# Stacked attention operands by per-block copies and doubled transposes, and half of a softmax's scalings on ScalarE, in a hybrid encoder layer

## The chip, the cores and the metric

The kernel runs on one core of one Trainium2 chip. The metric is the device time of one execution, in microseconds (us). TensorE (PE) multiplies matrices, VectorE (DVE) and ScalarE (ACT) do elementwise work, GpSimd (POOL) here raises small vectors to a power and issues DMA transfers that can add to what lies in the destination, and SyncE (SP) issues plain DMA loads.

## The reference

One layer of a bidirectional encoder on 512 tokens of width 1024, in float32. A vector `c` gives shift, scale and gate for three sublayers:

```python
x = x + 0.5 * g1 * swiglu(modulate(rmsnorm(x)), w_ffn1_in, w_ffn1_out)
h = modulate(rmsnorm(x))
qa, ka, va, qb, kb, vb, ga, gb = split(h @ w_in)
# mixer A: 8 query heads, 2 key heads of 64, keys within 128 positions, a sink in the softmax
ya = window_gqa_sink(rope(rmsnorm(qa)), rope(rmsnorm(ka)), va, sink) @ w_branch_a
# mixer B: 4 heads, two softmaxes each (64 wide), softmax_0 - lam * softmax_1, values 128 wide
yb = rmsnorm(diff_attention(rope(rmsnorm(qb)), rope(rmsnorm(kb)), vb, lam)) * 0.8 @ w_branch_b
x = x + g2 * ((sigmoid(ga) * ya + sigmoid(gb) * yb) @ w_out)
x = x + 0.5 * g3 * swiglu(modulate(rmsnorm(x)), w_ffn2_in, w_ffn2_out)
```

## The kernel before

All big products are made in a split form. A float32 operand is held as a high part, rounded to the format that TensorE multiplies, and a low part, the rest. A product is then three matmuls: high by high, high by low, low by high. `split_from` (L168) makes the parts: ScalarE copies the source to the high part (L169), VectorE subtracts to get the low part (L170). `load_split` (L194) does this for a weight of 128 by 1024 that SyncE has loaded into a `raw` tile. `load_main` (L1063) does it otherwise: ScalarE writes the high part (L1068) and the negated high part into the low tile (L1069), and a GpSimd DMA (L1070) adds the same weight from DRAM to it, so VectorE has no part in it. Weights in split form stand in one of five places (`high_low`, L175), which a holder can reserve.

The scores of both mixers use stacked operands instead. A head is 64 wide, and TensorE contracts over 128 partitions. One operand carries the high part of a head on partitions 0 to 63 and its low part on partitions 64 to 127; the other carries a head doubled. Two matmuls with full height then do what three would do with half height (L1293, L1451).

The middle of the kernel works like this. `main` (L1543) is a stream of projections, gate products and branch products, and yields an estimated cost after each step. `Line` (L47) keeps an estimated clock and a list of pieces of attention work with due times; when the clock passes a due time, the piece is put into the program there. Pieces also ask that a PSUM bank be free by the estimate (`line.free`). In this part the order on each engine is not the program's: a scheduler with its own model of times orders the instructions by what is ready. Buffers are tiles with a tag and a fixed number of slots; a tile that finds no free slot waits. PSUM banks: three of tag "acc", three of "sc", one "tp", one "op".

- `project` (L1116) multiplies the normalised input with a projection's weight into four banks (three "acc", one "sc"), one for each block of 128 tokens.
- `keys_b` (L1236): for each of four blocks, `keys` (L1209) norms and rotates the keys, and `turn_heads` (L1191) transposes four pairs of heads on TensorE (`turned`, L1179, in the bank "tp") and splits the result. So `kb[0]` first holds high parts of both heads of a pair (on partitions 0 to 63 and 64 to 127), and `kb[1]` the low parts. After the last block three GpSimd copies, each of 64 partitions by 2048 elements (512 KB), exchange halves by way of a spare tile (L1242 to L1244), each after the one before: then `kb[0]` holds high and low part of the first heads, `kb[1]` those of the second.
- `queries_b` (L1254), which follows the next projection, doubles the queries by a ScalarE copy; `query_turn` (L1265) transposes them, and `diff_scores` (L1278) runs the score products, 16 units in all, with gate products (`gates`, L1140) as filler work between the pieces.
- `queries_a` (L1420): for each of four blocks the queries of mixer A are transposed and split into two tiles of tag "f2" (eight slots), and four GpSimd copies of 64 partitions by 512 elements (128 KB, L1427) put high and low parts of each key head's queries into `wa["q"]`. After block 0 the first window scores are due 5.5 us after the estimate of the bank "tp" being free.
- `window_scores` (L1437), eight units of four score products, each followed by a softmax: scores with the mask (L1454), the maximum and the sink (L1465 to L1468), four exponentials on ScalarE (L1471), sums and reciprocals (L1475, L1476), and four scalings by the reciprocal on VectorE (L1478). `window_turn` transposes the probabilities, `window_out` multiplies with the values.
- Beside the window stage run the rest of the gates, the branch of mixer B (`w_yb`), and the first half of the branch of mixer A (`w_ya`, tokens 0 to 255, L1539); its second half waits until all window units are done. `load_ya` (L1573) loads the four weights of `w_ya` by `load_split` and keeps them for both halves.

Then come the product with `w_out`, and the second SwiGLU, where the order is written out by hand.

Of the kernel before, what the change touches and what calls it, by code (L numbers as in the profile page):

```python
# [18 lines left out]
P = 128  # L19
# [105 lines left out]
def layer(ctx: ExitStack, tc: tile.TileContext, a: dict):  # L125
# [934 lines left out]

    hh, hl = new_h()

    def load_main(src):  # L1063

        raw = sbuf("raw", [P, 1024], F32, RAW)
        nc.sync.dma_start(raw, src)
        hi, lo = high_low()
        S.copy(hi, raw)  # L1068
        S.activation(lo, raw, AF.Identity, scale=-1.0)  # L1069
        G.dma_start(lo, src, accum_op=ALU.add)  # L1070
        return hi, lo
# [119 lines left out]
    def turn_heads(srcs, hi, lo):  # L1191
        v = turned(srcs).rearrange("p (j q) -> p j q", j=len(srcs))
        split_from(hi, lo, v)

    def raws(ps, n=T):
# [3 lines left out]
            S.copy(out[-1], p[:, 0:n])  # L1199
        return out  # L1200

    def queries(ps, tabs, rq, outs, then):
        for t, raw in enumerate(raws(ps)):
            z = head_stats(raw, 8, rq[:, t, :], True)
            y = rope(raw, 8, tabs, t, z, outs and outs[t])
            due = line.helped(2.6, 2.5) + SLACK
            line.at(due, lambda y=y, t=t: then(y, t), ("tp",))
# [27 lines left out]

    def keys_b(ps):  # L1236
        def then(y, ht):
            hi, lo = kb
            turn_heads(cut(y, 4), hi[:, :, ht], lo[:, :, ht])
            if ht.stop == T:  # L1240
                spare = ob_h[0:HD]
                G.dma_start(spare, hi[HD:P])  # L1242
                G.dma_start(hi[HD:P], lo[0:HD])
                G.dma_start(lo[0:HD], spare)  # L1244

        for t, raw in enumerate(raws(ps)):
            keys(raw, 8, table["kb"], t, then)
# [172 lines left out]
    def queries_a(ps):  # L1420
        def then(y, t):
            ht = slice(t * P, (t + 1) * P)
            both = [sbuf("f2", [P, 4, P], F32R, F2) for _ in range(2)]
            turn_heads(cut(y, 4), *both)
            for kv in range(2):
                for j in range(2):
                    G.dma_start(wa["q"][kv][j * HD : (j + 1) * HD, :, ht], both[j][kv * HD : (kv + 1) * HD])  # L1427
            if t == 0:
                line.at(line.free["tp"] + 5.5, lambda: window_scores(0, 0, 0, None), ("sc0", "sc1"))

        queries(ps, table["qa"], wa["rq"], None, then)

# [4 lines left out]
    def window_scores(b, kv, g, st):  # L1437
        rqa = wa["rq"]
        first, nk = span(b)
        n = nk * P  # L1440
        mo = (first - (b - 1)) * P
        bq = slice(b * P, (b + 1) * P)
        bk = slice(first * P, first * P + n)
        unit = 2 * b + kv
        if g == 0:
            wide = b8(F32) if unit % 3 == 2 else None
            st = (small(4), [], line.now, wide)
        mx, sc, start, wide = st
        s_ps = bank("sc")
        for j in range(2):  # L1450
            PE.matmul(s_ps[:, 0:n], wa["q"][kv][:, g, bq], wa["k"][j][:, kv, bk], start=j == 0, stop=j == 1)  # L1451
        line.now += MM3 * 2 / 3 * n / T
        s = xt() if wide is None else wide[:, g, :]
        V.tensor_tensor_reduce(  # L1454
            out=s[:, 0:n], in0=s_ps[:, 0:n], in1=wa["mask"][:, mo : mo + n], scale=1.0, scalar=TINY,
            op0=ALU.add, op1=ALU.max, accum_out=mx[:, g : g + 1],
        )
        line.free[f"sc{(4 * unit + g) % 3}"] = line.helped(0.5, 0.3)
        sc.append(s)
        if g < 3:  # L1460
            line.at(line.now, lambda: window_scores(b, kv, g + 1, st), (f"sc{(4 * unit + g + 1) % 3}",))
            return
        den, nm, es = small(4), small(4), small(4)
        sk = sink[:, kv * 4 : kv * 4 + 4]
        V.tensor_tensor(nm, mx, rqa[:, b, kv:8:2], ALU.mult)  # L1465
        V.tensor_tensor(nm, nm, sk, ALU.max)
        V.tensor_tensor(es, sk, nm, ALU.subtract)
        V.tensor_scalar(nm, nm, -1.0, None, ALU.mult)  # L1468
        S.activation(es, es, AF.Exp)
        for q in range(4):  # L1470
            S.activation(  # L1471
                sc[q][:, 0:n], sc[q][:, 0:n], AF.Exp, bias=nm[:, q : q + 1],
                scale=rqa[:, b, 2 * q + kv : 2 * q + kv + 1], accum_out=den[:, q : q + 1],
            )
        V.tensor_tensor(den, den, es, ALU.add)  # L1475
        V.reciprocal(den, den)  # L1476
        for q in range(4):
            V.tensor_scalar(sc[q][:, 0:n], sc[q][:, 0:n], den[:, q : q + 1], None, ALU.mult)  # L1478
        due = line.helped(0.5, 3.2)
        due = line.helped(1.3, 0.5, due)  # L1480
        line.at(due + SLACK, lambda: window_turn(b, kv, 0, sc), (turn_tag(b, kv, 0),))
        nxt = (b, 1) if kv == 0 else (b + 1, 0)
        if nxt[0] < NT:
            line.at(
                start + PERIOD_A, lambda: window_scores(*nxt, 0, None),
                (f"sc{(4 * unit + 4) % 3}", lambda: unit - turns["a"] < DEPTH_A),
            )
# [55 lines left out]
    def main():  # L1543
        yield from project(vb_w, T, values_b)
        yield from project(a["w_kb"], T, keys_b, load_split, 1)
        yield from project(a["w_qb"], T, queries_b, load_split, 2)
        yield from gates(lambda: done["b"] < NT)
        line.drain(lambda: done["b"] == NT)
        start_a()
        again()  # L1550
        yield from project(a["w_kva"], 256, keys_a, load_half, 3)
        yield from project(a["w_qa"], T, queries_a, load_split, 3)
        yield from gates()
        ma = [b8(F32) for _ in range(2)]

        def then_a(j, g, y, r):
            V.scalar_tensor_tensor(ma[j // 4][:, j % 4, r], g, 1.0, y, ALU.add, ALU.mult)
            line.helped(0.6)

        yield from branch(a["w_yb"], 8, ob_h, ob_l, then_a, load_main)  # L1560
        mix.extend(new_h())
        mh, ml = mix

        def then_b(j, g, y, r):
            V.scalar_tensor_tensor(g, g, 1.0, y, ALU.add, ALU.mult)
            m = ma[j // 4][:, j % 4, r]
            V.tensor_tensor(m, m, g, ALU.add)
            split_from(mh[j][:, r], ml[j][:, r], m)
            line.helped(1.0)

        w_ya = {}

        def load_ya(u):  # L1573
            if u in w_ya:
                let_go(("ya", u))
            else:
                w_ya[u] = load_split(a["w_ya"][u], aside=ASIDE, holder=("ya", u))
            return w_ya[u]

        for i, r in enumerate(HALVES):  # L1580
            line.drain(lambda: done["a"] >= 2 * i + 2)
            yield from branch(range(4), 0, *wa["o"], then_b, load_ya, r)
# [377 lines left out]
```

## Time and profile before

| | |
|---|---|
| median of 3 runs | 1082.35 us (1080.17 to 1082.73) |
| the profiled execution's own time | 1081.27 us |
| span of its trace | 1079.5 us |
| mean granted TensorE clock | 0.99 |
| PE busy | 1046.5 us (97%), 7184 matmuls |
| VectorE busy | 801.4 us (74%) |
| ScalarE busy | 572.5 us (53%) |
| GpSimd busy | 155.8 us (14%) |
| DMA | 215.65 MB, mean 200 GB/s |

The profile shows one execution. A row of the timeline gives start, duration, engine, line, operation, output and input names, and in brackets the engine's idle time before it with what ended that. Rows of the waits give who waited for whom: total, number of times, longest. The granted clock is the share of TensorE's full clock. Rows of POOL's or SP's DMA instructions are the issues; a transfer lands later. "DMA b<-b" in a wait is a transfer's landing.

### The profile page before, as it was taken

How to read it: one execution, taken by the hardware profiler on the slowest of the kernel's cores; microseconds unless marked ns; L12 is line 12 of the kernel's file. 1: busy time of each engine (PE TensorE's matmuls, PEld its weight loads, DVE VectorE, ACT ScalarE, POOL GpSimd, SP SyncE). 2: the span in 40 equal slices, each digit the busy share in tenths (PEclk: the TensorE clock that was granted, in tenths of full speed). 3: DMA queues.
4: the chain of work that ended last, by engine and by line, in shares of the span. 5: the costliest groups of instructions: out<-in, count | busy, mean ns of one | idle time of the engine just before them, and what ended most of it. 6: DMA issues, size and time to landing. Idle time of an engine off the chain costs nothing.

```text
span 1079.5 us, 18400 instructions
## 1 busy us (share of the span) xinstructions
PE 1046.5 (97%) x7184; PEld 956.2 (89%) x7184; DVE 801.4 (74%) x1449; ACT 572.5 (53%) x938; POOL 155.8 (14%) x181
## 2 busy tenths in 40 slices
PE   8999999999999999979999899899999999999998
PEld 6799899889998988857887778789999999999997
DVE  7987877687867755647963589885878777877877
ACT  5566235425554534658645366434765645655553
POOL 1100001010101102411002700101021111211210
PEclk9999999999999999989999999899999999999999
DMA  9967887697776294963458961884397999998974
GB/s 350 372 154 227 270 211 188 200 278 203 177 220 216 101 350 121 207 149 89 124 175 198 230 164 61 304 286 79 78 206 172 235 240 238 184 231 210 222 150 122
DMA packets 68777, 215.65 MB, mean 200 GB/s; under 512 B 7953, under 2 KB 14225, under 8 KB 68498
## 3 DMA queue, kind: packets, MB, share of 16 engines
q1 hardware_dynamic: 43920, 143.63, 39.0%
q0 software_dynamic: 22320, 66.60, 34.1%
q10 hardware_dynamic: 2450, 4.25, 1.1%
q8 instruction: 56, 0.92, 0.3%
q14 instruction: 31, 0.25, 0.1%
HBM read 201.86 MB, written 8.92 MB: 195 GB/s over the span
## 4 chain that ended last, share of the span: by engine, by line
PE 73%; issue 8%; DVE 7%; DMA 6%; ACT 3%; POOL 2%; ACTq 0%; SPq 0%; DVEq 0%; POOLq 0%
PE acc L434 5%; PE acc L435 5%; PE acc L436 5%; PE sc L166 5%; PE sc L165 5%; PE sc L164 5%; PE sc L434 5%; PE sc L436 5%; PE sc L435 5%; PE acc L165 2%; PE acc L164 2%; PE acc L166 2%; PE acc L1132 2%; PE acc L1134 2%; PE acc L1133 2%
## 5 line engine op out<-in xcount | busy, mean ns | idle before, releaser
L434 PE MATMUL acc<-b,high 128*128 128x256 f32 x614 | 170.7, 278 | 0.4 <-DVE f L504 0.2
L436 PE MATMUL acc<-b,low 128*128 128x256 f32 x614 | 170.5, 278 | 0.1
L435 PE MATMUL acc<-b,high 128*128 128x256 f32 x614 | 170.4, 278 | 0.2 <-DVE b L1744 0.2
L169 ACT CAST high<-raw 128x1024 fp32r<-128x1024 f32 (+1 forms) x92 | 94.6, 1032 | 120.1 <-PE sc L1134 19.0
L434 PE MATMUL sc<-b,high 128*128 128x256 f32 x550 | 152.4, 277 | 1.3 <-ACT f L502 1.2
L436 PE MATMUL sc<-b,low 128*128 128x256 f32 x550 | 152.4, 277 | 0.1
L435 PE MATMUL sc<-b,high 128*128 128x256 f32 x550 | 152.1, 277 | 0.0
L170 DVE TENSOR_TENSOR low<-raw,high 128x1024 fp32r<-128x1024 f32 (+1 forms) x92 | 109.9, 1199 | 51.4 <-ACT high L169 51.0
L434 PEld LDWEIGHTS acc<-b,high 128*128 128x128 f32 x614 | 115.8, 189 | 0.8 <-DVE f L504 0.4
L435 PEld LDWEIGHTS acc<-b,high 128*128 128x128 f32 x614 | 116.0, 189 | 0.5 <-DVE b L1744 0.4
L436 PEld LDWEIGHTS acc<-b,low 128*128 128x128 f32 x614 | 115.8, 189 | 0.4 <-DVE low L170 0.3
L434 PEld LDWEIGHTS sc<-b,high 128*128 128x128 f32 x550 | 103.3, 188 | 1.7 <-ACT f L502 1.7
L436 PEld LDWEIGHTS sc<-b,low 128*128 128x128 f32 x550 | 103.3, 188 | 0.5 <-DVE low L786 0.3
L435 PEld LDWEIGHTS sc<-b,high 128*128 128x128 f32 x550 | 103.3, 188 | 0.0
L164 PE MATMUL sc<-b,high 128*128 128x512 f32 (+1 forms) x272 | 99.1, 364 | 0.0
L166 PE MATMUL sc<-b,low 128*128 128x512 f32 (+1 forms) x272 | 98.8, 363 | 0.2 <-DVE low L880 0.2
L165 PE MATMUL sc<-b,high 128*128 128x512 f32 (+1 forms) x272 | 99.0, 364 | 0.0
L169 ACT CAST high<-u 128x1024 fp32r<-128x1024 f32 (+1 forms) x51 | 52.2, 1025 | 44.3 <-PE acc L435 12.3
L164 PE MATMUL acc<-b,high 128*128 128x512 f32 (+1 forms) x200 | 74.4, 374 | 0.7 <-ACT b L169 0.7
L165 PE MATMUL acc<-b,high 128*128 128x512 f32 (+1 forms) x200 | 73.1, 366 | 0.0
L166 PE MATMUL acc<-b,low 128*128 128x512 f32 (+1 forms) x200 | 73.0, 365 | 0.0
L170 DVE TENSOR_TENSOR low<-u,high 128x1024 fp32r<-128x1024 f32 (+1 forms) x51 | 60.8, 1191 | 15.2 <-ACT high L169 14.6
(387 smaller groups left out, 2705.2 us busy)
## 6 DMA issues: line engine op xcount, KB each, us to landing
u<-w_mod SPq DMA_DIRECT2D x66, 512.0 KB, 7.1
raw<-w2i SPq DMA_DIRECT2D x31, 512.0 KB, 5.3
u<-w2i POOLq DMA_DIRECT2D x31, 512.0 KB, 7.0
raw<-w1u SPq DMA_DIRECT2D x27, 512.0 KB, 5.1
u<-w1u POOLq DMA_DIRECT2D x18, 512.0 KB, 8.0
raw<-w1o SPq DMA_DIRECT2D x16, 512.0 KB, 3.9
raw<-w_gate SPq DMA_DIRECT2D x16, 512.0 KB, 4.4
low<-w_gate POOLq DMA_DIRECT2D x13, 512.0 KB, 7.3
```

The costliest lines, as they stand in the source:

```text
L164: PE.matmul(out, wh, xh, start=first, stop=False)
L165: PE.matmul(out, wh, xl, start=False, stop=False)
L166: PE.matmul(out, wl, xh, start=False, stop=last)
L169: S.copy(hi, src)
L170: V.tensor_tensor(lo, src, f(hi), ALU.subtract)
L434: PE.matmul(out, wh[:, s], xh, start=first and j == 0, stop=False, skip_group_check=True)
L435: PE.matmul(out, wh[:, s], xl, start=False, stop=False, skip_group_check=True)
L436: PE.matmul(out, wl[:, s], xh, start=False, stop=last and j == 1, skip_group_check=True)
L1132: PE.matmul(out[t][:, 0:n], hh[k][:, ht], wh[:, o : o + n], start=k == 0, stop=False)
L1133: PE.matmul(out[t][:, 0:n], hh[k][:, ht], wl[:, o : o + n], start=False, stop=False)
L1134: PE.matmul(out[t][:, 0:n], hl[k][:, ht], wh[:, o : o + n], start=False, stop=k == NC - 1)
```

## The change

- `keys_b` and `queries_a` call one new function, `stack`. For blocks that are not "direct" it transposes four pairs of heads into both halves of one tile of tag "u4" (six slots) and issues four GpSimd copies of 128 KB, one for each of two outputs and of high and low part. For a direct block (`direct`: the last block of the keys, the first block of the queries) it doubles every head by two ScalarE copies, makes four transposes for each of the two outputs (in the banks "tp" and "acc"), copies the result to all 128 partitions of the output on ScalarE, and subtracts on VectorE on partitions 64 to 127 alone, so that the low part lies there. It issues no DMA.
- The three exchanging copies of the keys are gone; in their place stand twelve copies of 128 KB for blocks 0 to 2. Of the queries' sixteen copies twelve remain.
- The first window scores are due 1.0 us after the estimate of the bank "tp" being free, not 5.5.
- Two of each unit's four scalings move to ScalarE.
- `w_ya` is loaded by `load_main`, so its low parts are made by ScalarE and a GpSimd DMA of 512 KB each.

```diff
-    def load_main(src):
+    def load_main(src, aside=0, holder=None):
 
         raw = sbuf("raw", [P, 1024], F32, RAW)
         nc.sync.dma_start(raw, src)
-        hi, lo = high_low()
+        hi, lo = high_low(aside=aside, holder=holder)
         S.copy(hi, raw)
         S.activation(lo, raw, AF.Identity, scale=-1.0)
         G.dma_start(lo, src, accum_op=ALU.add)
...
+    def stack(outs, y, ht, direct):
+        if not direct:
+            t = u4()
+            both = [t[:, j, :].rearrange("p (h q) -> p h q", h=4) for j in range(2)]
+            turn_heads(cut(y, 4), *both)
+            for i, out in enumerate(outs):
+                for j, part in enumerate(both):
+                    G.dma_start(out[j * HD : (j + 1) * HD, :, ht], part[i * HD : (i + 1) * HD])
+            return
+        t = u4(F32).rearrange("p a (h w d) -> p (a h) w d", w=2, d=HD)
+        for w in range(2):
+            S.copy(t[:, :, w, :], y.rearrange("p (h d) -> p h d", d=HD))
+        for i, out in enumerate(outs):
+            v = turned([t[:, 2 * h + i].rearrange("p w d -> p (w d)") for h in range(4)], ("tp", "acc")[i])
+            v = v.rearrange("p (h q) -> p h q", h=4)
+            S.copy(out[:, :, ht], v)
+            V.tensor_tensor(out[HD:P, :, ht], v[HD:P], f(out[HD:P, :, ht]), ALU.subtract)
...
     def keys_b(ps):
         def then(y, ht):
-            hi, lo = kb
-            turn_heads(cut(y, 4), hi[:, :, ht], lo[:, :, ht])
-            if ht.stop == T:
-                spare = ob_h[0:HD]
-                G.dma_start(spare, hi[HD:P])
-                G.dma_start(hi[HD:P], lo[0:HD])
-                G.dma_start(lo[0:HD], spare)
+            stack(kb, y, ht, ht.stop == T)
...
             ht = slice(t * P, (t + 1) * P)
-            both = [sbuf("f2", [P, 4, P], F32R, F2) for _ in range(2)]
-            turn_heads(cut(y, 4), *both)
-            for kv in range(2):
-                for j in range(2):
-                    G.dma_start(wa["q"][kv][j * HD : (j + 1) * HD, :, ht], both[j][kv * HD : (kv + 1) * HD])
-            if t == 0:
-                line.at(line.free["tp"] + 5.5, lambda: window_scores(0, 0, 0, None), ("sc0", "sc1"))
+            stack(wa["q"], y, ht, t == 0)
+            if t:
+                return
+            line.at(line.free["tp"] + 1.0, lambda: window_scores(0, 0, 0, None), ("sc0", "sc1"))
...
         for q in range(4):
-            V.tensor_scalar(sc[q][:, 0:n], sc[q][:, 0:n], den[:, q : q + 1], None, ALU.mult)
+            if q % 2:
+                S.mul(sc[q][:, 0:n], sc[q][:, 0:n], den[:, q : q + 1])
+            else:
+                V.tensor_scalar(sc[q][:, 0:n], sc[q][:, 0:n], den[:, q : q + 1], None, ALU.mult)
...
-                w_ya[u] = load_split(a["w_ya"][u], aside=ASIDE, holder=("ya", u))
+                w_ya[u] = load_main(a["w_ya"][u], ASIDE, ("ya", u))
```

## The prediction

> **What bounds the kernel now.** I read the page's busy shares first, then the waits by releaser for the stretches that the diff touches, then the timelines of TensorE and GpSimd around each long wait, and last the windows table for the granted clock.
>
> ```profile
> span 1079.5 us, 18400 instructions
> PE 1046.5 (97%) x7184; PEld 956.2 (89%) x7184; DVE 801.4 (74%) x1449; ACT 572.5 (53%) x938; POOL 155.8 (14%) x181
> ```
>
> TensorE (PE) is busy for 97% of the span, so only two things are to be had: its 33 us of idle time, and time in which it is busy at a lower clock. No other engine's load counts by itself. The diff works between the second mixer's keys (about 430 us) and the gate products that follow the first mixer's attention (about 690 us), so I looked for idle time there.
>
> ```profile
> PE sc L1293 <- DMA b<-b: 7.0, 2, 6.0
> ...
> 444.43 0.56 POOL L1242 DMA_DIRECT2D b<-b  x1 [2.63 <-ACT b L169]
> ...
> 451.77 6.62 POOL L1162 TENSOR_TENSOR rqb<-rqb,half 128x8 f32<-128x8 f32 x3
> ```
> ```profile
> 451.21 8.65 DMA b<-b
> ...
> 460.15 7.93 DMA b<-b
> ```
> ```profile
> 460.00 0.70 PE L1293 MATMUL sc<-b,b 128*128 128x512 f32 x2 [0.99 <-DMA b<-b]
> ...
> 468.12 1.22 PE L1293 MATMUL sc<-b,b 128*128 128x512 f32 x2 [6.04 <-DMA b<-b]
> ```
>
> First place. The three copies that restack the keys (L1242 to L1244) run one after another: 6.8 us from 444.43, then 8.65 and 7.93. The first score product waits 0.99 us for the second copy and the next one 6.04 us for the third, with all gate products queued behind them on PE.
>
> ```profile
> 597.68 0.60 PE L1183 MATMUL tp<-ident,f 128*128 128x128 f32 x4
> ...
> 612.20 0.36 PE L1451 MATMUL sc<-ka,b 128*128 128x256 f32 x1 [3.40 <-DMA b<-f]
> ```
> ```profile
> 673.68 0.28 PE L1451 MATMUL sc<-u,b 128*128 128x256 f32 x1
> ...
> 682.31 0.33 PE L1183 MATMUL acc<-ident,x 128*128 128x128 f32 x1 [1.11 <-DVE x L1478]
> ...
> 684.16 0.50 PE L164 MATMUL op<-u,b 128*128 128x512 f32 x1 [0.62 <-ACT u L169]
> ...
> 688.00 1.01 PE L164 MATMUL acc<-b,high 128*128 128x256 f32 x3 [0.68 <-ACT b L169]
> ```
>
> Second place: the first block of the first mixer's queries is transposed at 597.68, and its first window score starts at 612.20, after 3.40 us of waiting for the copies of L1427. Third place: from the last window score (673.68) to the products that need the finished attention (688.00) lie 14.3 us; the filler work runs out, and PE idles for 1.11, 0.62 and 0.68 us.
>
> ```profile
> 468.10:473.40 5.30, 5.28 (x15) 4.23 (x16) 1.01 (x3) 1.45 (x3) 0.00 (x0) 0.51 0.45 90
> 500.00:550.00 50.00, 48.78 (x276) 39.86 (x275) 43.69 (x114) 34.99 (x88) 3.98 (x4) 1.00 0.45 125
> 600.00:640.00 40.00, 35.61 (x170) 28.54 (x168) 24.22 (x79) 17.95 (x41) 13.76 (x20) 0.96 1.10 228
> 613.30:616.70 3.40, 3.40 (x12) 2.82 (x11) 2.71 (x8) 0.82 (x2) 2.17 (x4) 0.50 2.22 233
> 640.00:700.00 60.00, 57.27 (x364) 50.27 (x363) 52.12 (x160) 34.01 (x82) 4.32 (x8) 0.94 0.47 167
> 680.80:685.00 4.20, 2.25 (x12) 1.11 (x11) 3.77 (x13) 2.00 (x6) 1.70 (x4) 1.00 0.39 103
> 685.00:691.80 6.80, 6.12 (x22) 5.11 (x23) 3.06 (x6) 0.58 (x1) 0.43 (x1) 0.50 1.01 394
> ```
>
> The columns are the stretch and its length, then busy time of PE, PEld, DVE, ACT and POOL, the granted clock, the DMA share and GB/s. After each of the three idle spells PE works at half clock: 5.28 us at 0.51, 3.40 at 0.50, 6.12 at 0.50. Work done at half clock would have taken half the time, so the spells cost a further 2.6, 1.7 and 3.1 us. In full the three places cost 7.03 + 2.6 = 9.6 us, 3.40 + 1.7 = 5.1 us, and 2.41 + 3.1 = 5.5 us.
>
> **Keys of the second mixer.** The chain of three large copies goes. Blocks 0 to 2 are split into a side tile, and each is carried over by four copies of 128 KB that depend on nothing but their own block. Block 3 isn't copied: its heads are doubled by two ScalarE copies, turned by eight transposes instead of four, and split in place by two ScalarE copies and two VectorE subtractions.
>
> ```profile
> L1427 POOL DMA_DIRECT2D b<-f x16: 608/657/1332, 602.6 to 617.5; - x16
> ...
> DMA to landing us min/median/max: 5.0/8.2/11.8
> ```
> ```profile
> POOL b L1427 <- DMA b<-f: 3.1, 1, 3.1
> ```
> ```profile
> 429.98 0.44 PE tp L1183 x4
> ```
> ```profile
> 441.96 0.59 ACT L1199 COPY f<-acc 128x512 f32<-128x512 f32 x1
> ...
> 452.49 0.62 ACT L1256 COPY b<-b 128x512 f32<-128x512 f32 x1
> ```
> ```profile
> 442.09 0.69 DVE L170 TENSOR_TENSOR b<-tp,b 128x512 fp32r<-128x512 f32 x1 [2.35 <-ACT b L169]
> ...
> 458.51 0.68 DVE L170 TENSOR_TENSOR b<-acc,b 128x512 fp32r<-128x512 f32 x1
> ```
>
> L1427 is a copy of the very shape that the keys now get. Block 2's split ends at 442.8 (442.09 + 0.69). Four issues of 0.66 us follow on POOL, so the last copy leaves at 445.4 and lands between 450.4 (5.0 us) and 457.2 (11.8 us); with the 3.1 us that this queue once waited for earlier copies of its own, at 460.3 at worst. It is needed when the first turned queries are split, at 459.2 (458.51 + 0.68), perhaps two us earlier, because the power operations (L1162) had stood in POOL's queue behind the second large copy until 451.77 and no longer do. So the wait left over is 0 to about 3 us. I take 1.0, since the median landing (8.2) gives 453.6 to 456.7.
>
> The second set of four transposes needs a bank of the tag "acc", and the query projection holds all three. That is a new wait, on the copy out of the first of them, over at 442.6 (441.96 + 0.59); PE's next accumulations and the gates would be queued behind it. The third turned block stood at that point anyway, so I take it at nothing; if the cover fails, the loss is one bank's turn, about 0.5 us. PE's added work is four transposes, 0.44 us. The net three added ScalarE copies (0.62 each) and one subtraction lie beside PE's projection. POOL issues twelve copies instead of three, 5.9 us more, past the gates' loads and the power operations; the wait for the first copy to land, which held that queue before, is gone. Gain: 9.6 - 0.4 - 1.0 = 8.2 us, between 5.5 and 9.2.
>
> **Queries of the first mixer.** Block 0 goes the direct way and needs no copy; the planner puts its scores 1.0 us behind the transposes instead of 5.5. From 597.68 I count two doublings (1.24), eight transposes (0.88), two copies (1.24) and the last subtraction (0.69): ready at about 601.7. PE had other work until 608.8 (612.20 - 3.40), 7 us of cover, so the wait and its half-clock spell go, for 0.44 us of transposes. Blocks 1 to 3 keep their copies with four fewer ahead of them, and block 1 is wanted only two score units later. Gain: 5.1 - 0.4 = 4.7, taken as 4.6.
>
> **The end of the window stage.** The same edit lets the first scores start 7 us of PE work earlier than the remaining filler. The shortfall at the end runs from 680.8 to 688.0, also 7 us. If the score units kept their pace, all 5.5 us would go; but the pace is set by a planner and by chains through four engines. I take 3.0, bounds 0 and 5.5.
>
> **Scalings and the loads of w_ya.**
>
> ```profile
> L1478 DVE TENSOR_SCALAR x<-x,sm 128x256 f32<-128x256 f32 x16 | 4.5, 348 | 0.0
> ...
> L1478 DVE TENSOR_SCALAR x<-x,sm 128x384 f32<-128x384 f32 x8 | 2.8, 415 | 0.0
> L1478 DVE TENSOR_SCALAR b<-b,sm 128x384 f32<-128x384 f32 x8 | 2.8, 416 | 0.0
> ```
> ```profile
> 669.63 0.41 ACT L169 CAST b<-b 128x256 fp32r<-128x256 f32 x1
> ```
> ```profile
> L1069 ACT ACTIVATE low<-raw 128x1024 fp32r<-128x1024 f32 x16 | 17.0, 1061 | 9.8 <-PE sc L1133 9.7
> L170 DVE TENSOR_TENSOR low<-raw,high 128x1024 fp32r<-128x1024 f32 x12 | 14.6, 1220 | 4.8 <-ACT high L169 4.8
> ```
> ```profile
> ACT sm L1469 <- DVE sm L1467: 12.6, 5, 6.2
> ...
> L1471 ACT ACTIVATE x<-x,sm,rqb 128x256 f32<-128x256 f32 x16 | 9.4, 590 | 0.3 <-DVE sm L1468 0.2
> ```
>
> Sixteen of 32 scalings leave VectorE, half of 10.1 us, and four low parts of 1.22, together 10 us. ScalarE gets sixteen at 0.41 to 0.59 us and four of 1.06, about 12 us. VectorE was the fuller one (52.12 against 34.01 of 60 us). Within a unit, two scalings on each engine take about 0.9 us in place of 1.14 in a row. It is worth -1 to +1 us to the end; I take nothing. [...]
>
> The sum is 8.2 + 4.6 + 3.0 = 15.8 us. The profiled execution took 1081.27 us, which gives 1065.5. That run lies 1.1 below the median of 1082.35 (three runs, 1080.17 to 1082.73); I forecast 1066.
>
> **Rivals.** *Late keys.* If the copies land at 465, because twelve small ones share POOL's queue with gate loads and wait for each other, PE idles 5 us and the clock halves again: the first place returns 9.6 - 5 - 2.6 - 0.4 = 1.6, and the time is 1081.3 - 1.6 - 4.6 - 3.0 = 1072. For it: 3.1 us of just such waiting in L1427. Against: 2.5 to 5.6 us between the median landing and the need. That the clock halves even after short spells is shown at 682 us, where no gap exceeds 1.11 us. [...]
>
> *Transfers become the bound.* From 600 to 640 the DMA share is 1.10 at 228 GB/s. The change adds four transfers of 512 KB (w_ya's low parts) and takes away four of 128 KB, 1.6 MB or 7 us at that rate. If gate loads and these collide, the second and third place return nothing: 1081.3 - 8.2 = 1073. Against: from 640 on the share is 0.47, and w_ya isn't needed at once.
>
> *Given back.* PE's wait at 462 let VectorE catch up, which is busy 43.69 of 50 us at 500 to 550. Were it the true pace of these stages, PE would wait for it later and the time stay at 1081. Against: PE is busy 48.78 there.
>
> *Slower.* A scaling on ScalarE queues behind whatever stands there; if that is the next unit's four exponentials (0.59 each and more), each unit's chain grows by up to 3 us. There are eight units. The first 7 us in all are the cover that the earlier start won, and cost just the third gain; past that PE stands idle. It decides from (7 + 12.8) / 8 = 2.5 us per unit; at 3.0 the kernel takes about 1086. Against: ScalarE itself waited 12.6 us for VectorE in this stage.
>
> **Numbers.** Forecast 0.66, late keys 0.12, transfers 0.12, given back 0.04, slower 0.06. Faster by over 0.3% (about what a measurement of this kernel can tell from no change, 3 us) holds the first three, 0.90; same 0.04; slower 0.06. The forecast's own range is 1061 (all bounds good: 9.2 + 4.7 + 5.5 and a good run) to 1070; taking in both partial rivals, 1060 to 1076.
>
> **What would show it.** Right: no wait of the first score products (L1293's) for DMA over 2 us, and a granted clock of 1.00 there; first window scores within 5 us of the transposes, on no transfer; less idle time and half clock before the second half of the last branch. Wrong: PE waiting on the small copies, GpSimd held by them; window score units farther apart than 8.8 us ((673.68 - 612.20) / 7); gate loads landing later than before; or PE's idle time reappearing under other names with the same sum.

## The result and the profile after

The kernel after took 1070.39 us (median of 5 runs, 1067.82 to 1072.62), the kernel before 1081.66 us beside it (5 runs, 1078.54 to 1082.73). The ratio is 0.9901, with a 95% interval of 0.9875 to 0.9926: faster by 1%. The time lies 0.4 us above the forecast's own range (1061 to 1070) and inside the wider one (1060 to 1076); the gain is 11.3 us where the terms summed to 15.8. The profiled execution took 1070.39 us with a span of 1068.6.

The head of the page of the kernel after:

```profile
span 1068.6 us, 18434 instructions
PE 1039.5 (97%) x7192; PEld 953.0 (89%) x7192; DVE 793.6 (74%) x1431; ACT 586.8 (55%) x964; POOL 163.4 (15%) x190
```

PE is busy 7.0 us less, with eight matmuls more. Less of the work ran at half clock: 18.2 us of PE's busy time before, 8.7 after, which is 4.8 of the 7.0 us. To see where the time went, I cut both spans at three marks that the two programs share: the first product of mixer B's projections, the last row of score products of mixer B, and the first product of the second SwiGLU (L434).

| stretch | before, us | after, us | gain | predicted |
|---|---|---|---|---|
| up to mixer B's projections | 378.1 | 377.5 | 0.6 | 0 |
| projections to last score of mixer B (keys) | 159.3 | 153.3 | 6.0 | 8.2 |
| from there to the second SwiGLU (queries 4.6, end of window stage 3.0) | 208.7 | 203.5 | 5.3 | 7.6 |
| second SwiGLU, untouched | 333.5 | 334.4 | -1.0 | 0 |

The gains add to the 10.9 us between the spans. Both middle stretches gained, and both less than forecast. Each stretch is from one execution: in traces of the experiments below that leave a stretch untouched, the keys' came out up to 2.0 us shorter than before and the next one up to 3.0 us longer, so the split between the rows is good to 2 or 3 us.

**Keys.** The rows of PE that have an idle time there now, or stand for the disputed bank (timeline of the kernel after; in brackets the idle time and what ended it):

```profile
441.34 0.66 PE L1183 MATMUL tp<-ident,f 128*128 128x128 f32 x4 [2.11 <-DVE u L170]
...
444.14 0.60 PE L1183 MATMUL tp<-ident,u 128*128 128x128 f32 x4
444.57 0.60 PE L1183 MATMUL acc<-ident,u 128*128 128x128 f32 x4
...
462.37 0.97 PE L1305 MATMUL sc<-b,b 128*128 128x512 f32 x3 [1.70 <-DVE b L170]
```

Before, the first scores waited 0.99 and 6.04 us for transfers. Now no score product waits for a transfer, and the two sets of doubled transposes run back to back without waiting for the bank "acc". But two waits for VectorE have come, 2.11 and 1.70 us. What VectorE itself waited for:

```profile
438.73 1.35 DVE L269 CUSTOM_DVE_ANT_0 u<-u,ka,begin 128x1024 f32<-128x1024 f32 x1 [3.92 <-DMA u<-w_mod]
...
460.83 0.17 DVE L1275 TENSOR_SCALAR nrqb<-rqb 128x8 f32<-128x8 f32 x1 [2.38 <-POOL rqb L1162]
460.91 0.68 DVE L1176 TENSOR_TENSOR b<-f,f 128x512 f32<-128x512 f32 x1
461.62 0.69 DVE L170 TENSOR_TENSOR b<-acc,b 128x512 fp32r<-128x512 f32 x1
```
```profile
451.07 7.17 POOL L1162 TENSOR_TENSOR rqb<-rqb,half 128x8 f32<-128x8 f32 x3 [0.87 <-DVE rqb L1159]
458.19 0.91 POOL L1070 DMA_DIRECT2D low<-w_gate  x1
458.82 1.97 POOL L1162 TENSOR_TENSOR rqb<-rqb,half 128x8 f32<-128x8 f32 x1
```

The first wait: VectorE stood 3.92 us at a column of the modulation (L269), whose weight had been loaded too late. That weight and the keys' new side tiles share the tag "u4" of six slots. The issue of the last such weight ahead of this place, after and before (SyncE, and for the kernel after the first copies of key blocks on GpSimd):

```profile
402.36 26.50 SPq L1066 DMA_DIRECT2D raw<-w_gate  x6
428.91 0.43 SPq L234 DMA_DIRECT2D u<-w_mod  x1
...
431.10 1.32 POOL L1209 DMA_DIRECT2D b<-u  x2
```
```profile
396.05 0.42 SPq L234 DMA_DIRECT2D u<-w_mod  x1
```

The load left 33 us later than before, right behind six gate loads in SyncE's queue, and 2.2 us ahead of the first copy of a key block. So no copy's landing held it: its place in the order of the queue changed. That the shared tag is why is shown by the runs below that give the side tiles another one. The subtraction that PE needs (L170) stood behind that column. The second wait: VectorE's next instruction was the negation of a scale (L1275), and that scale's power is GpSimd's fourth, which ends at 460.8. The split of the turned queries, which the first scores need, stood behind the negation until 461.62. Before, the same negation (L1263 there) waited no less, but VectorE had run the split at 458.51, ahead of it; the order of the two is new:

```profile
462.43 0.17 DVE L1263 TENSOR_SCALAR nrqb<-rqb 128x8 f32<-128x8 f32 x1 [2.64 <-POOL rqb L1162]
```

**Queries and the window stage.** First PE, then ScalarE and VectorE around its new idle time:

```profile
591.23 0.66 PE L1183 MATMUL tp<-ident,u 128*128 128x128 f32 x4
591.72 0.60 PE L1183 MATMUL acc<-ident,u 128*128 128x128 f32 x4
...
597.42 0.27 PE L1460 MATMUL sc<-ka,b 128*128 128x256 f32 x1
...
626.75 0.69 PE L1460 MATMUL sc<-ka,b 128*128 128x384 f32 x1 [5.53 <-DVE sm L1463]
```
```profile
623.97 0.59 ACT L169 CAST u<-tp 128x512 fp32r<-128x512 f32 x1 [8.13 <-DMA b<-u]
```
```profile
624.59 0.69 DVE L170 TENSOR_TENSOR u<-tp,u 128x512 fp32r<-128x512 f32 x1 [7.74 <-ACT u L169]
```

The direct block does what it was priced for: from its transposes to the first window score are 6.2 us in place of 14.5 (612.20 - 597.68; the prediction named 5 as a sign of being right), and nothing waits for a transfer there. Thirty microseconds later something else does. ScalarE wants to write the high part of the transposed probabilities, the tile `pt` of `window_turn`, and waits 8.13 us until a *copy of the queries has landed*: `pt` has the tag "u4", and one of its slots is still held by a side tile of a query block. VectorE stands behind ScalarE, the scores' bank isn't read, and PE idles 5.53 us. GpSimd shows why that copy was late, and the row of L1209 (all copies of side tiles) what it cost:

```profile
607.91 0.63 POOL L1209 DMA_DIRECT2D b<-u  x1 [1.12 <-ACT low L1069]
609.68 0.61 POOL L1209 DMA_DIRECT2D b<-u  x1 [1.14 <-DMA b<-u]
611.59 0.61 POOL L1209 DMA_DIRECT2D b<-u  x1 [1.30 <-DMA b<-u]
613.40 0.61 POOL L1209 DMA_DIRECT2D b<-u  x1 [1.20 <-DMA b<-u]
```
```profile
L1209 POOL DMA_DIRECT2D b<-u x24: 608/618/1004, 431.1 to 613.4; - x24
...
  ACT u L169: 8.1, 1
...
DMA to landing us min/median/max: 5.5/9.4/12.5
```

The last block's four copies leave one by one, three of them after a wait for an earlier one to land; the last leaves at 613.40 and lands 10.4 us later, just before ScalarE goes on. ScalarE had begun to write its block's side tile at 603.89: one tile held a slot for 20 us.

The windows of the kernel after (columns as in the prediction):

```profile
457.00:463.00 6.00, 4.30 (x22) 3.28 (x20) 2.94 (x11) 4.05 (x7) 3.79 (x3) 1.00 0.94 226
600.00:640.00 40.00, 34.47 (x170) 28.81 (x168) 21.74 (x79) 26.55 (x62) 9.26 (x14) 0.91 0.93 209
...
625.19:632.02 6.83, 5.27 (x14) 4.30 (x15) 5.22 (x23) 5.52 (x14) 0.00 (x0) 0.50 0.34 88
678.00:690.00 12.00, 11.93 (x100) 11.76 (x101) 12.00 (x32) 6.58 (x11) 0.00 (x0) 1.00 1.03 383
```

The clock is whole at the first scores of mixer B, where it was 0.51, and at the end of the window stage, where 6.8 us ran at half. The new idle time brings 6.83 us of half clock of its own, 2.6 us lost on 5.27 us of work. At the end of the window stage only one wait over 0.3 us is left on PE:

```profile
678.07 0.39 PE L165 MATMUL acc<-b,high 128*128 128x256 f32 x1 [1.13 <-DVE b L170]
```

### The profile page after: what moved, and what is told of

Read it like the earlier page. It is cut to its first block, busy times and chain, and to the rows that moved or that the text cites. A ratio compares the mean times of both kernels' runs of the same rounds, so it can differ in the third digit from the quotient of the medians.

```text
span 1068.6 us, 18434 instructions
## 1 busy us (share of the span) xinstructions
PE 1039.5 (97%) x7192; PEld 953.0 (89%) x7192; DVE 793.6 (74%) x1431; ACT 586.8 (55%) x964; POOL 163.4 (15%) x190
## 4 chain that ended last, share of the span: by engine, by line
PE 66%; issue 12%; DMA 10%; DVE 7%; ACT 2%; POOL 2%; SPq 0%; POOLq 0%; DVEq 0%; ACTq 0%
PE acc L434 4%; PE acc L436 4%; PE acc L435 4%; PE sc L166 4%; PE sc L164 4%; PE sc L165 4%; PE sc L434 4%; PE sc L436 4%; PE sc L435 4%; PE acc L165 3%; PE acc L164 3%; PE acc L166 3%; DMA u<-w2i 3%; DMA b<-u 2%; PE acc L1134 2%
## 5 line engine op out<-in xcount | busy, mean ns | idle before, releaser
L434 PE MATMUL acc<-b,high 128*128 128x256 f32 x614 | 170.8, 278 | 0.4 <-DVE f L504 0.2
L434 PE MATMUL sc<-b,high 128*128 128x256 f32 x550 | 152.4, 277 | 2.6 <-ACT f L502 2.4
L169 ACT CAST high<-raw 128x1024 fp32r<-128x1024 f32 (+1 forms) x88 | 90.4, 1031 | 115.1 <-PE sc L1134 19.2
L170 DVE TENSOR_TENSOR low<-raw,high 128x1024 fp32r<-128x1024 f32 (+1 forms) x88 | 105.0, 1197 | 51.7 <-ACT high L169 51.3
L434 PEld LDWEIGHTS acc<-b,high 128*128 128x128 f32 x614 | 115.8, 189 | 1.0 <-DVE f L504 0.4
L434 PEld LDWEIGHTS sc<-b,high 128*128 128x128 f32 x550 | 103.3, 188 | 3.2 <-ACT f L502 2.8
L269 DVE CUSTOM_DVE_ANT_0 u<-u,ka,begin 128x1024 f32<-128x1024 f32 x48 | 62.5, 1309 | 16.8 <-DMA u<-w_mod 16.7
L164 PE MATMUL acc<-b,high 128*128 128x512 f32 (+1 forms) x200 | 73.1, 365 | 0.0
L170 DVE TENSOR_TENSOR low<-u,high 128x1024 fp32r<-128x1024 f32 (+1 forms) x51 | 60.7, 1191 | 16.6 <-ACT high L169 16.1
L165 PE MATMUL acc<-b,high 128*128 128x512 f32 (+1 forms) x200 | 71.9, 360 | 1.1 <-DVE b L170 1.1
```

Source lines behind the costliest of these rows:

```text
L164: PE.matmul(out, wh, xh, start=first, stop=False)
L165: PE.matmul(out, wh, xl, start=False, stop=False)
L169: S.copy(hi, src)
L170: V.tensor_tensor(lo, src, f(hi), ALU.subtract)
L269: summed = V.tensor_tensor_reduce(out=w, in0=w, in1=cact, scale=by, scalar=b, op0=ALU.mult, op1=ALU.add, accum_out=t,)
L434: PE.matmul(out, wh[:, s], xh, start=first and j == 0, stop=False, skip_group_check=True)
```

## Experiments

My theory after the result: the change's parts do what they should, and what is missing is lost by *where the side tiles lie*. A side tile holds its slot until its copies land, so a tag that other users need makes them wait (5.53 us and a half-clock spell in the window stage; the 2.11 us in the keys were put down to the same, though the rows above show there a load that moved back in a queue and no landing); 1.70 us more is the negation behind GpSimd. Rivals: the stall in the window stage comes from `w_ya`'s low parts, which now go by GpSimd's queue; or from the scalings on ScalarE. Diffs are against the kernel after unless they say otherwise.

**The side tile in the tag "f2"**, where the queries' tiles were before.

```diff
-            t = u4()
-            both = [t[:, j, :].rearrange("p (h q) -> p h q", h=4) for j in range(2)]
+            both = [sbuf("f2", [P, 4, P], F32R, F2) for _ in range(2)]
```

> The changed kernel, but the side tile of the copied blocks stands in two tiles of tag f2 (as the queries' did before) instead of one of tag u4. Theory 'slots': both new waits of the changed kernel come from u4's six slots. TensorE's 2.1 us at 441 (VectorE behind a column of w_mod whose load was queued late) and its 5.5 us at 627 (ScalarE's copy of turned probabilities waiting for a u4 tile until query copies land) go, with about 2.6 us of half clock behind the second: some 10 us less, about 1060 us. Theory 'transfers': the copies are late because the DMA engines are full, whatever tile they leave from; the waits stay or move to f2's users (the loads from gate_scr), about 1070 us. Theory 'w_ya': its four added transfers hold the query copies up; then nothing changes here either, about 1070 us.

Measured: 1069.57 us, ratio 0.9899 (0.9877 to 0.9921) beside 1080.23 us of the kernel before (29 runs). That is nearly the time of the kernel after, as 'transfers' had it, and not the 1060 us of 'slots'; the waits are other ones. The 5.53 and the 2.11 us are gone. In their place the rotation of mixer B's queries, whose tiles have the tag "f2", waited for the keys' copies (VectorE, then PE, of this kernel):

```profile
447.24 0.69 DVE L1172 TENSOR_TENSOR f<-f,Cqb 128x512 f32<-128x512 f32 x1 [3.39 <-DMA b<-f]
449.70 0.69 DVE L1172 TENSOR_TENSOR f<-f,Cqb 128x512 f32<-128x512 f32 x1 [1.76 <-DMA b<-f]
```
```profile
463.05 0.96 PE L1304 MATMUL sc<-b,b 128*128 128x512 f32 x3 [3.06 <-DVE b L170]
```

The keys' stretch grew from 153.3 to 156.0 us, and the one from there to the second SwiGLU fell from 203.5 to 199.6. So each tag has its victim: "u4" in the window stage, "f2" in the keys. Since 'transfers' allowed for waits at the users of "f2", this run alone doesn't tell the theories apart; the second group below does.

**Each part alone.** Three kernels start from the kernel before. One has the new keys only (`stack` in `keys_b`), one the new queries only (`stack` in `queries_a`, due 1.0), one the scalings and `load_main` for `w_ya` only.

> The kernel before with the new keys alone (queries, scalings and w_ya as before). All theories: the waits of 0.99 and 6.04 us and their half clock (9.6 us) go, 0.44 us of transposes come. 'Slots': the waits of 2.1 and 1.7 us stay, so 5 to 6 us less than before, about 1076 us. 'Transfers' and 'w_ya': both late waits are of the query stage or the load there, so the keys alone give the 8 us that the prediction wrote down, about 1073.5 us.

Measured: 1075.7 us, 0.9961 (0.9945 to 0.9977). The keys' stretch gained 5.9 us, as in the kernel after, with waits of 1.77 and 1.70 us at the same two places. The rest up to the second SwiGLU, which this kernel doesn't touch, took 211.7 us in place of 208.7 and gave half of it back. Its trace shows a wait of PE for VectorE at 618.62 of 2.68 us (0.76 at this place in the kernel before), with a step of half clock behind it; VectorE had waited 4.48 us there for a gate load to land. The kernel with the last two edits alone has a like wait (2.71 us). Why it comes and goes is open.

> The kernel before with the new queries alone (keys, scalings and w_ya as before). 'Slots': the wait of 3.4 us and the end of the window stage are relieved (5.1 and 4.4 us), but the 5.5 us wait of window_turn's tile and its half clock (2.6) appear as in the changed kernel: 0 to 3 us less than before, about 1080 us, with a wait of ScalarE on a transfer of the query copies. 'Transfers': the same within 2 us. 'w_ya': without its four transfers the copies land in time and that wait is under 2 us: 7 to 9 us less than before, about 1073 us.

Measured: 1076.37 us, 0.9971 (0.9954 to 0.9988). The stall of the window stage is here as well, without the loads of `w_ya` by GpSimd and without the scalings on ScalarE (PE, then ScalarE, of this kernel; the profiled execution, 1082.06 us, was the second longest of 12):

```profile
631.96 0.69 PE L1466 MATMUL sc<-ka,b 128*128 128x384 f32 x1 [4.63 <-DVE sm L1469]
```
```profile
629.18 0.59 ACT L169 CAST u<-tp 128x512 fp32r<-128x512 f32 x1 [6.29 <-DMA b<-u]
```

Neither rival can be the cause of the stall with that: it comes with the queries' side tiles.

> The kernel before with the last two edits alone: half of the scalings on ScalarE and w_ya's low parts by transfer. 'Slots' and 'transfers': within 1 us of before (about 1081.5 us), since neither engine is the pace. 'w_ya': 2 to 4 us slower, the query copies land later and TensorE's wait at 612 us grows past 3.4 us.

Measured: 1079.86 us, 0.9987 (0.9972 to 1.0002). No effect that can be told from none.

**Slots that nobody waits for.** In a second group (kernel before: 1079.88 us, 11 runs) the side tiles are placed by use. First the keys' stay in "u4" and the queries' go to "f2".

```diff
-            t = u4()
-            both = [t[:, j, :].rearrange("p (h q) -> p h q", h=4) for j in range(2)]
+            if outs is kb:
+                t = u4()
+                both = [t[:, j, :].rearrange("p (h q) -> p h q", h=4) for j in range(2)]
+            else:
+                both = [sbuf("f2", [P, 4, P], F32R, F2) for _ in range(2)]
```

> The changed kernel with the keys' side tile in u4 (as it is) and the queries' in two f2 tiles. Theory 'held slots' (mended after the run with f2 in both places): a copy lands some 9 us after its issue, and the side tile keeps its slots until then; whoever needs that tag next waits: w_mod's column and window_turn for u4, the rotation of the queries and the gate loads for f2. Then the key stage keeps u4's waits (2.1 and 1.7 us) and the window stage has f2's (1.7 and 1.5 us, no half clock): about 1066 us. Theory 'late data': the consumers wait for the copied data itself, so the tag is of no account: about 1070 us.

Measured: 1066.47 us, 0.9864 (0.9837 to 0.989). In its trace the waits in the keys are left (1.59 and 1.70 us) and the 5.53 us is gone; among the window scores one wait of 0.93 us is left. That is 'held slots', and not 'late data'. Then the keys' go to the tag "x", whose eight slots are idle in this stage:

```diff
             if outs is kb:
-                t = u4()
-                both = [t[:, j, :].rearrange("p (h q) -> p h q", h=4) for j in range(2)]
+                both = [sbuf("x", [P, 4, P], F32R, 8) for _ in range(2)]
```

> As the run before, but the keys' side tiles stand in tag x, whose eight slots nobody uses in the key stage. 'Held slots': the 2.1 us wait at 441 goes as well, the 1.7 us wait of the first scores for the split of the queries stays: about 1064 us. 'Late data': about 1070 us.

Measured: 1063.54 us, 0.9839 (0.981 to 0.9869). The 2.11 and 5.53 us are both gone, the load of the modulation's weight leaves at 396.05 as before the change, and the granted clock is 1.00 over the whole span. Placing six tiles elsewhere brought some 7 us (0.9901 to 0.9839).

**The negated scales on GpSimd**, on top of that, so that VectorE doesn't stand behind GpSimd's power:

```diff
-            V.tensor_scalar(nrqb[:, t, :], rqb[:, t, :], -1.0, None, ALU.mult)
+            G.tensor_scalar(nrqb[:, t, :], rqb[:, t, :], -1.0, None, ALU.mult)
```

> The kernel of the run before, with the four small negations of the queries' scales (nrqb) on GpSimd instead of VectorE. They are what VectorE waits with in front of the first queries' split, for GpSimd's power of the fourth block. If that is the cause of the 1.7 us wait of the first scores, it goes: about 1062 us. Rival: the split is late for another reason (ScalarE's copy, the rotation), and the time stays that of the run before, about 1064 us.

Measured: 1062.5 us, 0.9839 (0.9809 to 0.9869). The times don't separate the two, and the ratio is that of the run before: in the time the edit brings nothing that shows. The trace does separate them. PE and GpSimd of this kernel:

```profile
457.91 1.07 PE L1307 MATMUL sc<-b,b 128*128 128x512 f32 x4
```
```profile
454.43 1.66 POOL L1162 TENSOR_TENSOR rqb<-rqb,half 128x8 f32<-128x8 f32 x1
456.18 0.24 POOL L1277 TENSOR_SCALAR nrqb<-rqb 128x8 f32<-128x8 f32 x1
456.64 0.94 POOL L1070 DMA_DIRECT2D low<-w_gate  x1 [0.23 <-ACT b L1270]
457.30 2.00 POOL L1162 TENSOR_TENSOR rqb<-rqb,half 128x8 f32<-128x8 f32 x1
```

The last power still ends at 459.3, but the scores start at 457.91 with no wait before them, and the stage from first to last score of mixer B is 68.45 us long in place of 70.49. In this trace the keys' stretch is 149.0 us, a gain of 10.3 on the kernel before, and the next one 198.6, a gain of 10.1; the untouched second SwiGLU took 338.1 us in it, 4.6 more than before.

**Every block direct**, without any copy: the other way to be rid of held slots.

```diff
-            stack(kb, y, ht, ht.stop == T)
+            stack(kb, y, ht, True)
...
-            stack(wa["q"], y, ht, t == 0)
+            stack(wa["q"], y, ht, True)
```

> The changed kernel with every block of keys and queries direct: no copy at all, 24 more transposes (2.6 us of TensorE), 18 more ScalarE copies of 0.6 us, six more subtractions. 'Held slots': with no transfer to wait for, the waits of 2.1 and 5.5 us and the half clock behind go (10.5 us less), the transposes come: about 1062 us. Rival 'engine queues': ScalarE, 11 us fuller in two short stretches, becomes what the transposes wait for, and the time is 1070 us or more.

Measured: 1070.35 us, 0.9906 (0.988 to 0.9932), no better than the kernel after. Up to the second SwiGLU it needs 730.6 us, 2.8 more than the kernel with copies in idle slots (727.8), which is about the price of 24 more transposes at 0.11 us (2.6; four took 0.44 in the kernel before). No wait for slots is left, so "held slots" was right on that and wrong on the sum. The time is what the rival 'engine queues' gave, but its mechanism isn't in the trace: from the keys to the end of the window scores PE's waits over 0.3 us are for VectorE, but for one of 0.8 us for ScalarE, which the kernel before has as well. The remainder of the 6.8 us between the medians lies at least in part in the second SwiGLU (336.9 us against 333.8 in the profiled runs), where PE waited 5.5 us against 1.7 for ScalarE at L502. Why an untouched stage does so is open; over the fourteen profiled executions of this document it took from 332.1 to 339.5 us.

**What each part is worth, from the best version.** The last group (kernel before: 1080.79 us, 11 runs) undoes one thing each in the version with idle slots and the negation on GpSimd. That version itself was measured in the group before (0.9839, 0.9809 to 0.9869), so the ratios to the kernel before are compared. First, the keys' last block copied like the others:

```diff
-            stack(kb, y, ht, ht.stop == T)
+            stack(kb, y, ht, False)
```

> Starts from the best version so far (side tiles in idle slots, negated scales on GpSimd; 0.984 of the kernel before, about 1062.5 us). Here the last block of the second mixer's keys is copied over like the first three, with no doubled transposes. 'Copies would do': with the chain of large copies gone and the slots free, four more small copies leave at about 447 and land 5.5 to 12.5 us later, at 452 to 459, and the first scores want them at 458: no wait over 1 us, 1062 to 1063 us. 'Direct block needed': the first score products wait 3 to 6 us for a transfer and the clock halves once, 1066 to 1070 us.

Measured: 1062.53 us, 0.9823 (0.98 to 0.9846). "Copies would do". GpSimd's last copy, then the first scores on PE, without a wait:

```profile
447.99 0.61 POOL L1211 DMA_DIRECT2D b<-x  x1 [0.18 <-issue]
```
```profile
458.34 0.84 PE L1307 MATMUL sc<-b,b 128*128 128x512 f32 x3
```

Second, the queries' first block copied like the others:

```diff
-            stack(wa["q"], y, ht, t == 0)
+            stack(wa["q"], y, ht, False)
```

> Starts from the same best version (about 1062.5 us). Here the first block of the first mixer's queries is copied over like the others. 'Direct block needed', by the prediction's second term: the first window score comes about 8 us later and waits 2 to 4 us for its transfer with a half-clock spell, and the window stage ends on less filler work: 1066 to 1070 us. 'Copies would do': other work of TensorE fills the time and only the order changes: 1062 to 1064 us.

Measured: 1071.01 us, 0.991 (0.9888 to 0.9931): with the direct block it is 0.7% faster. The due time stays 1.0 here, which places the first scores before a copied block is ready: the wait is 6.01 us, where the kernel before, with 5.5, had 3.40. A copied block with a due time of 5.5 was not run in this version, so what the direct block is worth beside that is open. Timeline of PE: transposes of that block, then its scores, here with a wait for the transfer and, from 597.25, 6.8 us of half clock.

```profile
586.66 0.60 PE L1183 MATMUL tp<-ident,f 128*128 128x128 f32 x4
...
601.03 0.58 PE L1462 MATMUL sc<-ka,b 128*128 128x256 f32 x1 [6.01 <-DMA b<-f]
```

Third, the scalings back on VectorE:

```diff
-            if q % 2:
-                S.mul(sc[q][:, 0:n], sc[q][:, 0:n], den[:, q : q + 1])
-            else:
-                V.tensor_scalar(sc[q][:, 0:n], sc[q][:, 0:n], den[:, q : q + 1], None, ALU.mult)
+            V.tensor_scalar(sc[q][:, 0:n], sc[q][:, 0:n], den[:, q : q + 1], None, ALU.mult)
```

> Starts from the same best version (about 1062.5 us). Here all four scalings of a window unit are on VectorE again. 'Off the path', as the prediction and the run of that part alone had it: 1061.5 to 1063.5 us. 'VectorE paces the units', now that other waits are gone: two more scalings of 0.35 to 0.42 us in each of 8 units, 0.75 us per unit, 6 us in all and a half-clock spell: 1067 to 1070 us.

Measured: 1061.51 us, 0.9822 (0.9797 to 0.9847): the same without them. Fourth, the direct block with the old due time of the first window scores:

```diff
-            line.at(line.free["tp"] + 1.0, lambda: window_scores(0, 0, 0, None), ("sc0", "sc1"))
+            line.at(line.free["tp"] + 5.5, lambda: window_scores(0, 0, 0, None), ("sc0", "sc1"))
```

> Starts from the same best version (about 1062.5 us). Here the planner places the first window scores 5.5 us after the transposes, as in the kernel before, instead of 1.0; the block still goes directly. 'The early start pays at the end of the window stage', the prediction's third term: the first score comes about 4.5 us later, and of that 2 to 4 us are lost as idle time and half clock before the second half of the last branch: 1064.5 to 1067 us. 'Only the order changes': the filler moves ahead of the scores and nothing is lost: 1062 to 1063.5 us.

Measured: 1066.99 us, 0.988 (0.9856 to 0.9904): 0.4% worse, which the intervals only just tell from nothing. The first scores come at 599.38 us here, at 593.24 in the version it starts from, and the rest up to the second SwiGLU doesn't catch up (729.7 against 725.0 us).

## Why the prediction was right in direction and too large

- **The bound** was read rightly: the gain lies in the two stretches that the change touches, and elsewhere no stretch moved by more than 1 us. Of their 11.3 us, 4.7 are idle time of PE and 4.8 work that no longer ran at half clock; the rest isn't accounted for.
- **Keys, 8.2 forecast, 6.0 measured.** The step that failed is "The wait left over is 0 to about 3 us", because it looked for that wait in the landing of the copies. The copies were in time: the last left at 445.5 and landed 5.5 us later. The waits that came, 2.11 and 1.70 us, were VectorE's. The side tile's use of "u4" slots was named in the description of the change and not priced at all; with it the load of a modulation weight moved behind gate loads. And the term took the first split to come at its old time or earlier, while in the new order it stands behind a negation that waits for GpSimd's fourth power. On the other side no half clock was left, and without the two waits this stretch gains 10.3 us, above the term's upper bound of 9.2, though the difference is within the 2 us by which the untouched stretch varies. (The 6.8 us that the prediction gives the first large copy is the time to the next issue; the copy landed after 6.2. No term rests on it.)
- **The bank "acc"** at nothing: right (444.14 and 444.57 follow each other).
- **The direct key block** was taken as needed, since its copies would come last. In the best version it is worth nothing that shows (0.9823 without it, 0.9839 with it); what paid was that the chain of three large copies went.
- **Queries 4.6 and end of the window stage 3.0, together 5.3 measured.** The mechanism was right: the wait for L1427 and the three idle spells at 682 to 688 went (one of 1.13 us is left), and copying the first block in the best version costs 0.7% or 7.7 us, against 7.6 forecast. That the two figures agree so well is partly luck, since that run keeps the early due time; the early due time alone is 0.4% or 4.4 us. The step that failed is "Blocks 1 to 3 keep their copies with four fewer ahead of them": it asked when the copies' *results* are wanted, not when their *source tile* is. A slot held until the landing gave back 5.53 us of idle time and 2.6 of half clock. That is a wait in the place of one removed, and none of the four rivals was it. By the number alone *Late keys* (1072) and *Transfers* (1073) came closer than the forecast, with mechanisms that the trace doesn't show.
- **Scalings and `w_ya`** at nothing: right, shown alone (0.9987) and in the best version (0.9822 without the scalings). In the kernel after a scaling takes longer on ScalarE than on VectorE (two in a row take 0.91 us there and 0.62 us on VectorE, 128 by 256); here neither place is on the path.
- **Rivals.** Late keys: no score waited for a copy. Transfers: the DMA share from 600 to 640 fell from 1.10 to 0.93, and new places for the side tiles removed the stall, so what bit was a slot. How much of the copies' time to land (median 9.4 us, 8.2 before) is due to full DMA engines was not separated. Given back and slower: no. Of the signs of being wrong, GpSimd did wait for small copies to land (3.6 us in three waits), units farther apart than 8.8 us did come, 9.1 ((661.4 - 597.42) / 7), because the stall lies among them, and "idle time reappearing under other names" came in part.

## What to carry to other kernels

A side tile, the source of DMA copies, held its slot here from the first write until the last copy had landed, up to 20 us, and as a new user of a tag it also moved another user's load back in a queue, by 33 us. So price such a tile for the next user of its tag, and put it into a tag that is idle at that time: that alone was worth more than half as much here as the whole change. When a long wait goes, read what stands on the waiting engine's *suppliers* just behind it: here a small instruction queued behind another engine's result was late next (a negation of 0.17 us that waited 2.38 us for a power on GpSimd); its removal took the wait out of the trace and nothing that shows out of the time. Then undo each part of a bundle in the final version: the direct query block with its early start carried a gain there, while the direct key block and the scalings carried none.

## What the runs showed of the clock

In the trace of the kernel before, spells of half clock start at 466.52, 613.29, 684.97 and 760.06 us, which is 43, 21 and 22 times 3.413 us apart, and last 6.83, 3.41, 6.83 and 3.41 us. In that of the kernel after they start at 625.19 and 748.07 us, 36 times 3.413 us apart, and last 6.83 and 3.41 us. (One more in each, at the very end of the span, is left out.) Windows of the kernel before, cut into steps of that length counted from the spells, at the end of its window stage:

```profile
681.56:684.97 3.41, 1.82 (x10) 1.08 (x10) 2.98 (x11) 1.38 (x3) 1.67 (x4) 1.00 0.29 62
684.97:691.80 6.83, 6.16 (x22) 5.14 (x23) 3.10 (x6) 0.58 (x1) 0.46 (x1) 0.50 1.02 396
```

And two steps of another trace, that of all query blocks copied, each with the step after it:

```profile
672.34:675.75 3.41, 1.81 (x16) 1.61 (x15) 3.31 (x6) 0.11 (x1) 0.00 (x0) 1.00 1.03 396
675.75:679.16 3.41, 3.41 (x33) 3.41 (x32) 1.14 (x5) 1.46 (x2) 0.00 (x0) 1.00 1.03 402
744.02:747.43 3.41, 1.81 (x13) 1.41 (x13) 2.43 (x4) 1.72 (x3) 0.00 (x0) 1.00 0.63 237
747.43:750.84 3.41, 3.41 (x18) 3.41 (x18) 2.41 (x6) 3.28 (x8) 0.00 (x0) 0.50 0.55 154
```

Three of these steps at full clock had PE busy for 1.81 or 1.82 us: half clock followed two of them, full clock the third. In the traces of the kernels before and after, cut in the same way, away from the first 20 us and the last 6, half clock followed six steps at full clock, with PE busy for 0.00, 1.09, 1.82 and 1.81 us before and 0.00 and 1.81 us after. It followed none of the others, of which the least busy had 1.77 us (437.46 of the kernel after) and 1.88 us (809.51). What tells steps of about 1.8 us apart is open; it isn't the number of matmuls in them (10 to 13 where half clock followed, 8 and 16 where it didn't). The gaps at the head of the untouched second SwiGLU were followed by 3.41 us of half clock in the traces of the kernel before, the kernel after and all query blocks copied (at 760.06, 748.07 and 747.43), which by an estimate, half of that stretch, cost up to 1.7 us each time. In the trace of the keys' side tiles in "x" and the queries' in "f2" the clock was 1.00 there. PE was busy for 1.81 us in one step ahead of the spell in each of the first three; in the fourth the gaps lay in two stretches of 3.41 us in a row, with 2.36 and 2.87 us (from 737.49). That the place of the gaps decides is a guess from these four traces; no run shows it.
